# A two-layer encoder trunk: background work of the FFN's up stage queued behind each product's copy and addition, left operands stepped by a schedule, and right-operand sums formed between rows

## The chip, the cores and the metric

The kernel runs on one core of a Trainium2 chip. The metric is the device time of one execution in microseconds (us); the figure given for a kernel is the median of several runs.

The engines are named as in the profile. PE is TensorE: its matmuls write PSUM, and its weight loads are PEld. DVE is VectorE and ACT is ScalarE. POOL is GpSimd. SP issues the DMAs. Each engine takes its own instructions in a fixed order, and semaphores hold an instruction back until its inputs and its output buffer are free.

## What is computed

A tensor of 1024 tokens by 1024 features runs through two layers. Each layer adds a mixer (a state-space group and a differential attention group) and then a gated FFN with a causal convolution over three tokens. The part that matters here:

```python
def _conv_gated_ffn(h, w_up, w_conv, b_conv, w_down):
    up = h @ w_up
    padded = jnp.pad(up, ((0, 0), (CONV_WIDTH - 1, 0), (0, 0)))
    conv = b_conv + sum(w_conv[j] * padded[:, j:j + seqlen] for j in range(CONV_WIDTH))
    gate = conv[..., :FFN_DIM]
    val = conv[..., FFN_DIM:]
    return (jax.nn.silu(gate) * val) @ w_down

    # in the layer loop (DEPTH = 2, D_MODEL = SEQ = 1024, FFN_DIM = 2816)
    x = x + jnp.concatenate([y_ssm, y_att], axis=-1) @ w_out[i]
    h = _rmsnorm(x, norm_ffn[i])
    x = x + _conv_gated_ffn(h, w_up[i], w_conv[i], b_conv[i], w_down[i])
```

## The kernel before, in words

**Arithmetic.** A float32 matmul is made of three fp32r matmuls. `mm3` (lines 449 to 451) multiplies the rounded part ("hi") and the remainder ("lo") of both operands: hi by hi, hi by lo, lo by hi. A hi part is an ACT copy with rounding (`act`, line 97). A lo part is a subtraction: on POOL for weights (`split`, line 240), on DVE for most right operands (`Pieces.put`, line 472).

**The up stage.** `h @ w_up` is done with seven products in place of eight (the Strassen-Winograd form of a 2 by 2 block product). For each of the 22 tiles `f` of 128 FFN columns, the left blocks are gate and value columns by two halves of the features, and the right blocks are two halves of the features by two halves of the tokens. The right operands are seven sets of 512 features by 512 tokens, held as hi and lo: blocks 11, 21 and 22, and the sums t1 = 12 - 11, t2 = 22 - t1, t3 = 22 - 12, t4 = t2 - 21. One product is 4 feature tiles times three matmuls, so 12 matmuls of 128 by 512. `up(f)` runs the products 11, 12, s2, s1, s3, 22, s4 in this order into four PSUM tiles: `upa` takes 11, s2 and s3, each added to what stands there; `upb` takes 12; `upc` takes s1 and then s4 on top; `upd` takes 22. In between, ACT copies `upa` out into `u0` or `u1` after each of its three products, and DVE adds `upb`, `upc`, `upd` and `upc` again (line 100). The second product into `upa` or `upc` must not begin before the copy or addition that reads the first.

**Background work.** `bg` is a list of generators. `bg.tick()` lets each do one step, and `up` ticks after each product, seven times for one `f`. A step's instructions are written at the point of the tick, and the framework's scheduler then merges them, engine by engine, with the products' own copies and additions. Two kinds run here:

- `gate(f)` starts when `up(f)` ends. It makes the convolution of the value half (`c1`: one ACT operation, two DVE operations of line 106), of the gate half (`c0`), the silu on ACT and the multiplication into `g` on DVE.
- After every odd `f` up to 17, `spill` makes the seven left operands of the down stage out of two `g` tiles: sums on DVE (lines 317, 318, 328, 334), hi on ACT and lo on DVE (line 346) into tiles `ao`, which SP then stores to DRAM. It is a pipeline of three: at each tick one operand is summed, the previous one is rounded, the one before that gets its lo part. So it lies over the second half of an even `f` and all of the next odd `f`, together with the next gate.

POOL meanwhile makes the weights' sums and lo parts, seven products ahead of their use (`W.depth = 7`).

**The way into the up stage.** The output projection (`wo`) finishes token tiles `X[t]` of 128 rows, t = 0 to 7. After each odd t, `norm_ffn(tp)` norms two of them (tp = 0 to 3): squares on ACT, a Newton iteration on small DVE operations (`nw`, `rstd`), a scaling into `hn` (line 106). PE transposes `hn` (line 504) into PSUM tiles `nt`, and `put` writes hi and lo parts. For tp = 0 and 1 (tokens 0 to 511) these are the blocks 11 and 21. For tp = 2 and 3, `three(k)` takes the transposed blocks 12 and 22 out of PSUM and forms t1, t2 and t3 in tiles `ta` and `tb`, subtracting the hi and lo parts of 11 one after the other; t4 follows likewise (line 1320), on POOL for tp = 2. The products 11 and 12 of f = 0 and f = 1 need only tokens 0 to 511 and are run first, in front of

```python
        ups = [up(0), up(1)]
        for e in ups:
            next(e)
        bg.finish()
        W.fences.pop(0)
```

so all four norms are finished before `up(0)` goes on with its product s2.

Of the kernel before, what the change touches and what calls it, by code (L numbers as in the profile page):

```python
# [46 lines left out]
DN_ORDER = ["11", "12", "s2", "s3", "s1", "22", "s4"]  # L47
PARTNER = {"11": "11", "12": "21", "s4": "22", "22": "t4", "s1": "t1", "s2": "t2", "s3": "t3"}
# [3 lines left out]
def trunk_kernel(ctx: ExitStack, tc: tile.TileContext, A: dict, out: bass.AP, dbg: dict):  # L52
# [46 lines left out]
    def tt(o, a, b, op):  # L99
        V.tensor_tensor(o, a, b, op=op)  # L100
# [189 lines left out]
    class Seven:  # L290
# [49 lines left out]
        def spill(self, dst):  # L340

            todo, summed, rounded = list(DN_ORDER), None, None
            while todo or summed or rounded:
                if rounded:
                    (n, v, d), rounded = rounded, None
                    self.eng(n).tensor_tensor(d[:, 512:1024].bitcast(F32R), v, d[:, 0:512], op=SUB)  # L346
                    store(dst[n], d)
                if summed:
                    (n, v), summed = summed, None
                    d = s4("ao")  # L350
                    act(d[:, 0:512].bitcast(F32R), v, AF.Copy)
                    rounded = n, v, d
                if todo:
                    n = todo.pop(0)
                    summed = n, self.value(n)
                yield
# [131 lines left out]
    def norm_rows(xs, g, os, ps=None):  # L488

        n = len(xs)  # L490
        ss, y = few("ss", n), few("rstd", n)
        for i, (x, o) in enumerate(zip(xs, os)):
            squares.append(act(o, x, AF.Square, accum_out=ss[:, i:i + 1]))
# [4 lines left out]
    def turned(hs, k):  # L498

        n = 128 * len(hs)  # L500
        ps = bgt("nt")
# [685 lines left out]
    for l in range(DEPTH):  # L1187
# [86 lines left out]

        def norm_ffn(tp):

            rows_ = X[2 * tp:2 * tp + 2]
            hs = [s4("hn") for _ in rows_]
            norm_rows(rows_, gf, hs, mmt("nw") if tp == 3 else None)
            for s in range(2):  # L1280
                dma(xm[2 * tp + s], rows_[s])
            yield 1
            c, half = 256 * (tp % 2), tp // 2
            sums = G if tp == 2 else V

            def old(n, k, q):
                return B[n].tile(k, c)[q].rearrange("p (k n) -> p k n", k=2)[:, :, c:c + 256]

            def three(k):

                ta, tb = s4("ta"), s4("tb")
# [14 lines left out]
            if half == 0:  # L1306
# [256 lines left out]
```

## Time and profile before

| what | value |
|---|---|
| median of 3 runs | 2508.43 us (2503.97 to 2510.72) |
| the profiled execution | 2508.28 us, of which its span is 2506.5 us |
| PE busy | 2332.5 us (93% of the span) |
| PEld busy | 1931.1 us (77%) |
| DVE busy | 1758.8 us (70%) |
| ACT busy | 1111.8 us (44%) |
| POOL busy | 1163.4 us (46%) |
| mean granted TensorE clock | 0.979 of full speed |

The span is the time from the first to the last instruction. Busy time of PE counts overlapping matmuls once. A matmul's duration is longer than its share of the engine, since the next one starts before it ends; how fast PE goes is read from the distance between starts.

### The profile page before, as it was taken

The page shows a single profiled execution, that of the slowest core. Times are in us where ns is not written, and L with a number is a line of the kernel's source. Part 1 is how long each engine was busy: PE and PEld are TensorE (multiplying, and loading weights), DVE is VectorE, ACT ScalarE, POOL GpSimd, SP SyncE. Part 2 cuts the span into 40 slices and gives each one's busy share as a digit, 9 for nine tenths or more (in the row PEclk, how much of TensorE's full clock was granted, in tenths as well). Part 3 has the DMA queues.
Part 4 walks back from the last instruction along what each step waited for, and adds up shares of the span by engine and source line. Part 5 has one row for each costly group of instructions (what it writes and reads, how often), then busy time and mean ns, then how long its engine had stood idle before and what let it go on. Part 6 is the DMA issues. An engine that isn't in the chain of part 4 may idle for free. (4 is left out here: it accounts for less than half of the span.)

```text
span 2506.5 us, 34993 instructions
## 1 busy us (share of the span) xinstructions
PE 2332.5 (93%) x12180; PEld 1931.1 (77%) x12180; DVE 1758.8 (70%) x3273; ACT 1111.8 (44%) x2164; POOL 1163.4 (46%) x853
## 2 busy tenths in 40 slices
PE   5899999997999999999998999999979999999998
PEld 4777987785887777777787788877858777787776
DVE  7986567658777878456589775675677787864645
ACT  4455256434555555323135642754255555552221
POOL 3110011035777878778022101012277788878750
PEclk8999999999999999999999999999989999999999
DMA  6344741421344445786134447214114444549651
GB/s 179 119 115 116 196 120 47 149 82 51 109 148 130 161 134 176 296 305 236 53 101 153 116 135 216 70 51 156 68 42 143 135 155 139 167 161 367 225 180 68
DMA packets 295753, 361.42 MB, mean 144 GB/s; under 512 B 43160, under 2 KB 230136, under 8 KB 295576
## 3 DMA queue, kind: packets, MB, share of 16 engines
q1 hardware_dynamic: 295576, 359.18, 43.7%
q8 instruction: 97, 1.59, 0.3%
q14 instruction: 80, 0.66, 0.1%
HBM read 235.36 MB, written 123.73 MB: 143 GB/s over the span
## 5 line engine op out<-in xcount | busy, mean ns | idle before, releaser
L240 POOL TENSOR_TENSOR op<-st,op 128x512 fp32r<-128x512 f32 x112 | 169.5, 1541 | 886.5 <-ACT op L97 812.9
L240 POOL TENSOR_TENSOR op<-wu,op 128x512 fp32r<-128x512 f32 x220 | 325.1, 1499 | 160.9 <-ACT op L97 159.0
L106 DVE SCALAR_TENSOR_TENSOR c<-u,cv,c 128x1023 f32<-128x1023 f32 (+1 forms) x176 | 230.1, 1309 | 56.9 <-ACT c L97 52.8
L449 PE MATMUL rw<-op,hTh 128*128 128x256 f32 x768 | 228.8, 298 | 10.3 <-ACT hTh L97 3.5
L450 PE MATMUL rw<-op,hTh 128*128 128x256 f32 x768 | 225.8, 294 | 1.6 <-POOL op L240 1.6
L451 PE MATMUL rw<-op,hTl 128*128 128x256 f32 x768 | 224.1, 292 | 0.0
L100 DVE TENSOR_TENSOR xf<-xf,dnc 128x512 f32<-128x512 f32 (+1 forms) x160 | 124.7, 792 | 132.7 <-PE dnc L451 121.1
L240 POOL TENSOR_TENSOR op<-w,op 128x512 fp32r<-128x512 f32 x124 | 175.3, 1427 | 20.6 <-ACT op L97 20.5
L97 ACT ACTIVATE c<-u,cv 128x1024 f32<-128x1024 f32 x88 | 106.6, 1211 | 150.7 <-DVE u L100 144.0
L240 POOL TENSOR_TENSOR op<-wd,op 128x512 fp32r<-128x512 f32 x106 | 138.3, 1331 | 66.7 <-ACT op L97 66.7
L449 PEld LDWEIGHTS rw<-op,hTh 128*128 128x128 f32 x768 | 152.3, 198 | 12.9 <-ACT kr L97 4.6
L449 PE MATMUL dnc<-op,aop 128*128 128x512 f32 x360 | 146.0, 411 | 12.6 <-DVE xf L100 12.2
L450 PEld LDWEIGHTS rw<-op,hTh 128*128 128x128 f32 x768 | 152.2, 198 | 4.4 <-POOL op L240 2.3
L451 PEld LDWEIGHTS rw<-op,hTl 128*128 128x128 f32 x768 | 151.8, 198 | 0.7 <-issue 0.6
L450 PE MATMUL dnc<-op,aop 128*128 128x512 f32 x360 | 141.0, 392 | 0.0
L100 DVE TENSOR_TENSOR u<-u,upc 128x512 f32<-128x512 f32 x88 | 59.9, 681 | 115.3 <-ACT u L97 109.2
L97 ACT ACTIVATE u<-upa 128x512 f32<-128x512 f32 x132 | 78.0, 591 | 139.3 <-PE upa L451 137.2
L451 PE MATMUL dnc<-op,aop 128*128 128x512 f32 x360 | 139.1, 391 | 0.0
L97 ACT ACTIVATE op<-wu 128x512 fp32r<-128x512 f32 x220 | 128.9, 619 | 0.0
L346 DVE TENSOR_TENSOR ao<-g,ao 128x512 fp32r<-128x512 f32 x90 | 117.5, 1320 | 15.7 <-ACT ao L97 15.7
L97 ACT ACTIVATE op<-wd 128x512 fp32r<-128x512 f32 x106 | 62.2, 624 | 148.7 <-PE dnc L451 61.0
L97 ACT ACTIVATE e<-sc,anm 128x256 f32<-128x256 f32 (+7 forms) x128 | 94.1, 738 | 63.0 <-DVE anm L103 48.8
(346 smaller groups left out, 7124.0 us busy)
## 6 DMA issues: line engine op xcount, KB each, us to landing
wu<-in_w_up_dram SPq DMA_DIRECT2D x88, 512.0 KB
ad_s<-ao SPq DMA_DIRECT2D x72, 512.0 KB
aop<-ad_s SPq DMA_DIRECT2D x72, 512.0 KB
ad<-ao SPq DMA_DIRECT2D x54, 512.0 KB
aop<-ad SPq DMA_DIRECT2D x54, 512.0 KB
wd<-in_w_down_dram SPq DMA_DIRECT2D x44, 512.0 KB
st<-in_w_in_dram SPq DMA_DIRECT2D x32, 256.0 KB
st<-in_w_in_dram SPq DMA_DIRECT2D x16, 512.0 KB
```

Source lines behind the costliest of these rows:

```text
L97: return nc.scalar.activation(o, i, f, **kw)
L100: V.tensor_tensor(o, a, b, op=op)
L106: return V.scalar_tensor_tensor(o, a, s, b, op0, op1)
L240: eng.tensor_tensor(lo.bitcast(F32R), src, hi, op=SUB)
L346: self.eng(n).tensor_tensor(d[:, 512:1024].bitcast(F32R), v, d[:, 0:512], op=SUB)
L449: PE.matmul(o, l[0], r[0], start=first, stop=False, skip_group_check=go_on)
L450: PE.matmul(o, l[0], r[1], start=False, stop=False, skip_group_check=go_on)
L451: PE.matmul(o, l[1], r[0], start=False, stop=last, skip_group_check=go_on)
```

## The change

**Background.** A new function `behind()` ticks the background inside `tc.issue_after`: each instruction that the tick writes on ACT gets an order edge to the latest copy out of `upa`, each one on DVE an edge to the latest addition, so that the scheduler may not put it ahead of them. This holds once all norms are done. All ticks in `up` go through it.

**Left operands.** `spill` follows a table, `SPILL`: for each of nine ticks it lists which sums, hi and lo parts are made. The same 4 sums, 7 hi and 7 lo parts are made as before. The third and fourth ticks, which meet the convolutions of the next gate, are empty.

**Right operands.** The squares of a row tile are taken right after its last addition. For tp = 2 and 3 the sums t1, t2, t3 and t4 are formed between rows, before the transposition, in place in the `hn` tiles of tokens 0 to 511 (which are kept) and of tokens 512 to 1023, with t2 in the first of the two `X` tiles, whose store has been issued. Then all five blocks are transposed, so 10 groups of 8 transposes for these two tp where there were 4 of 8, through the wide PSUM tiles (`mmt`, two buffers). Every `put` now reads PSUM, all sums are on DVE.

**Order.** `up(0)` runs its products s2, s1, s3, 22 and s4 in two halves of 256 tokens, the first half as soon as tp = 2 is there, and the norms are finished after it.

```diff
+SPILL = [[("sum", "s1"), ("hi", "11")], [("sum", "s2"), ("lo", "11"), ("hi", "12")], [], [],
+         [("lo", "12"), ("sum", "s3"), ("hi", "s2")], [("lo", "s2"), ("sum", "s4"), ("hi", "s3")],
+         [("lo", "s3"), ("hi", "s1")], [("lo", "s1"), ("hi", "22"), ("hi", "s4")], [("lo", "22"), ("lo", "s4")]]
...
+            for step in SPILL:
+                for what, n in step:
+                    if what == "sum":
+                        o, p, q, op = sums[n]
+                        tt(o, p, q, op)
+                    elif what == "hi":
+                        d[n] = s4("ao")
+                        act(d[n][:, 0:512].bitcast(F32R), v[n], AF.Copy)
+                    else:
+                        tt(d[n][:, 512:1024].bitcast(F32R), v[n], d[n][:, 0:512], SUB)
+                        store(dst[n], d.pop(n))
                 yield
...
+            def put(n, src):
+                ps = mmt("nt") if tp > 1 else None
+                ps = [turned(src, k, ps and ps[:, 256 * k:256 * k + 512]) for k in (0, 2)]
                 for k in (0, 2):
-                    for n in ("11", "21"):
-                        B[n].put(k, 2, c, 256, turned(hs, k + 4 * (n == "21")))
+                    B[n].put(k, 2, c, 256, ps[k // 2])
...
+            for o, h, t2 in zip(ol, hs, e):
+                tt(o[:, lo], h[:, lo], o[:, lo], SUB)
+                tt(t2, h[:, hi], o[:, lo], SUB)
+            for o, h, t2 in zip(ol, hs, e):
+                tt(h[:, lo], h[:, hi], h[:, lo], SUB)
+            if tp == 2:
+                yield 1
+            for o, h, t2 in zip(ol, hs, e):
+                tt(o[:, hi], t2, o[:, hi], SUB)
+            yield 0 if tp == 2 else 2
...
+        def behind():
+
+            with ExitStack() as st:
+                for x in (emptied, added):
+                    if x and not any(e in bg.q for e in norms):
+                        st.enter_context(tc.issue_after(x[-1].ins))
+                bg.tick()
...
             product(a, "11", True)
-            act(u0[:, lo], a, AF.Copy)
-            bg.tick()
+            emptied.append(act(u0[:, lo], a, AF.Copy))
+            behind()
...
+            ws = W.take(5) if f == 0 else [None] * 5
+            for q, qn in ((0, 256), (256, 256)) if f == 0 else ((0, 512),):
+                v, x, y = slice(q, q + qn), slice(q, q + qn), slice(512 + q, 512 + q + qn)
+                product(a, "s2", False, ws[0], q, qn)
+                emptied.append(act(u0[:, y], a[:, v], AF.Copy))
+                behind()
...
+                product(a, "s3", False, ws[2], q, qn)
+                emptied.append(act(u1[:, x], a[:, v], AF.Copy))
+                added.append(tt(u1[:, y], u1[:, x], c[:, v], ADD))
+                behind()
...
         for e in ups:
             next(e)
-        bg.finish()
-        W.fences.pop(0)
-        for f in range(NF):
+        for e in ups[0]:
+            pass
+        bg.finish(*norms)
+        for f in range(1, NF):
```

Three places show what moves. The first is on DVE in f = 5 of the first layer, from the addition of `upb` to the addition of `upc` after which product s4 may begin. `w7` holds the sums s1 and s2, `g` the tiles of the gates (s3 and s4 are made in place in them), `ao` a left operand, `c0` and `c1` the convolutions. Before:

```order
L100 TENSOR_TENSOR u0_7479<-u0_7479,upb_7478 128x512
L328 TENSOR_TENSOR g_7271<-g_7271 128x512
L106 SCALAR_TENSOR_TENSOR c0_7533<-u0_7338,cv_4185,c0_7533 128x1022
L346 TENSOR_TENSOR ao_7530<-w7_7500,ao_7530 128x512
L346 TENSOR_TENSOR ao_7555<-g_7271,ao_7555 128x512
L346 TENSOR_TENSOR ao_7578<-w7_7500,ao_7578 128x512
L334 TENSOR_TENSOR g_7421<-g_7421,w7_7500 128x512
L100 TENSOR_TENSOR g_7580<-g_7580,c1_7503 128x1024
L100 TENSOR_TENSOR u1_7480<-u1_7480,upc_7557 128x512
```

Now (other line numbers, the same operations):

```order
L103 TENSOR_TENSOR u0_7580<-u0_7580,upb_7579 128x512
L109 SCALAR_TENSOR_TENSOR c1_7598<-u1_7480,cv_4185,c1_7598 128x1022
L109 SCALAR_TENSOR_TENSOR c0_7623<-u0_7432,cv_4185,c0_7623 128x1023
L103 TENSOR_TENSOR ao_7576<-g_7516,ao_7576 128x512
L109 SCALAR_TENSOR_TENSOR c0_7623<-u0_7432,cv_4185,c0_7623 128x1022
L103 TENSOR_TENSOR g_7363<-g_7363 128x512
L103 TENSOR_TENSOR ao_7646<-w7_7554,ao_7646 128x512
L103 TENSOR_TENSOR g_7516<-g_7516,w7_7554 128x512
L103 TENSOR_TENSOR u1_7627<-u1_7627,upc_7648 128x512
```

The gate's multiplication has moved behind the addition of `upc`; of the left operands five operations stood in front of it, now four stand there, with three convolution operations that ran earlier before.

The second place is on ACT at the start of f = 6. Before, the convolutions of f = 5 (`c1`, `c0`) stand ahead of the copy out of `upa` after product 11 (`op` are weights' hi parts):

```order
L97 ACTIVATE op104_7649<-wu_7367 128x512
L97 ACTIVATE c1_7666<-u1_7480,cv_4185 128x1024
L97 ACTIVATE c0_7691<-u0_7479,cv_4185 128x1024
L97 ACTIVATE u0_7647<-upa_7645 128x512
L97 ACTIVATE op105_7673<-wu_7513 128x512
```

Now:

```order
L100 ACTIVATE op104_7742<-wu_7461 128x512
L100 ACTIVATE u0_7741<-upa_7739 128x512
L100 ACTIVATE c1_7760<-u1_7627,cv_4185 128x1024
L100 ACTIVATE op105_7767<-wu_7608 128x512
L100 ACTIVATE c0_7785<-u0_7580,cv_4185 128x1024
```

The copy comes first, the convolutions behind it.

The third place is on DVE on the way into the up stage, at tp = 3. Before, for one of two pairs of feature tiles:

```order
L100 TENSOR_TENSOR ta_6763<-nt_6765,b11h_6370 128x512
L100 TENSOR_TENSOR ta_6763<-ta_6763,b11l_6371 128x512
L100 TENSOR_TENSOR ta_6763<-nt_6770,ta_6763 128x512
L100 TENSOR_TENSOR tb_6764<-nt_6770,tb_6764 128x512
L472 TENSOR_TENSOR bt1l_6605<-ta_6763,bt1h_6604 128x2x256
L472 TENSOR_TENSOR bt2l_6601<-ta_6763,bt2h_6600 128x2x256
L472 TENSOR_TENSOR bt3l_6609<-tb_6764,bt3h_6608 128x2x256
L472 TENSOR_TENSOR b22l_6613<-nt_6770,b22h_6612 128x2x256
```

Now, with sums for tp = 3 among the lo parts of tp = 2 (`xr` is the `X` tile that holds t2):

```order
L103 TENSOR_TENSOR hn_6353<-hn_6571,hn_6353 128x512
L103 TENSOR_TENSOR u0_6708<-u0_6708,upb_6707 128x512
L478 TENSOR_TENSOR bt3l_6735<-nt_6725,bt3h_6734 128x2x256
L103 TENSOR_TENSOR xr6_5865<-hn_6571,hn_6353 128x512
L103 TENSOR_TENSOR hn_6571<-hn_6571 128x512
L478 TENSOR_TENSOR bt3l_6739<-nt_6725,bt3h_6738 128x2x256
L478 TENSOR_TENSOR bt4l_6765<-nt_6755,bt4h_6764 128x2x256
L103 TENSOR_TENSOR hn_6352<-xr6_5865,hn_6352 128x512
```

The sums now read two tiles of rows, and each lo part reads a PSUM tile.

## Rows read from the trace of the kernel before

**Rows 1.** Windows, first layer: length; PE, PEld, DVE, ACT, POOL busy; clock; DMA share.

```profile
575.80:637.80 62.00, 46.48 (x194) 35.11 (x193) 51.29 (x67) 31.59 (x54) 42.23 (x29) 0.92 0.14 43
637.80:1031.00 393.20, 383.21 (x1668) 311.49 (x1667) 294.65 (x277) 207.48 (x321) 313.74 (x221) 1.00 0.44 147
```

**Rows 2.** Tile u of the whole span: who waited for it (us, times).

```profile
  PE upc L449: 18.9, 20
  PEld upa L449: 10.8, 18
```

**Rows 3.** Timeline of PE, f = 5 into f = 6: start, us, what, [idle before].

```profile
712.74 0.39 PE L451 MATMUL upd<-bt4h,op 128*128 128x512 f32 x1
714.04 0.50 PE L449 MATMUL upc<-b22h,op 128*128 128x512 f32 x1 [0.92 <-DVE u L100]
...
716.89 0.39 PE L449 MATMUL upa<-b11h,op 128*128 128x512 f32 x1
...
719.62 0.39 PE L449 MATMUL upb<-b21h,op 128*128 128x512 f32 x1
...
722.11 0.39 PE L451 MATMUL upb<-b21h,op 128*128 128x512 f32 x1
722.68 0.50 PE L449 MATMUL upa<-bt2h,op 128*128 128x512 f32 x1 [0.18 <-ACT u L97]
```

**Rows 4.** Timeline of DVE over the first of these two stalls.

```profile
703.59 0.68 DVE L100 TENSOR_TENSOR u<-u,upb 128x512 f32<-128x512 f32 x1
704.18 1.19 DVE L328 TENSOR_TENSOR g<-g 128x512 f32<-128x512 f32 x1
705.29 1.28 DVE L106 SCALAR_TENSOR_TENSOR c<-u,cv,c 128x1022 f32<-128x1022 f32 x1
706.48 0.68 DVE L346 TENSOR_TENSOR ao<-w,ao 128x512 fp32r<-128x512 f32 x1
707.09 1.78 DVE L346 TENSOR_TENSOR ao<-g,ao 128x512 fp32r<-128x512 f32 x1
708.79 1.77 DVE L346 TENSOR_TENSOR ao<-w,ao 128x512 fp32r<-128x512 f32 x1
710.49 1.77 DVE L334 TENSOR_TENSOR g<-g,w 128x512 f32<-128x512 f32 x1
712.18 1.21 DVE L100 TENSOR_TENSOR g<-g,c 128x1024 f32<-128x1024 f32 x1
713.32 0.67 DVE L100 TENSOR_TENSOR u<-u,upc 128x512 f32<-128x512 f32 x1
```

**Rows 5.** Timeline of POOL in the same stretch.

```profile
706.61 1.71 POOL L334 TENSOR_TENSOR wu<-wu,w 128x512 f32<-128x512 f32 x1
```

**Rows 6.** Timeline of ACT before the two stalls.

```profile
710.44 0.60 ACT L97 ACTIVATE u<-upa 128x512 f32<-128x512 f32 x1 [1.38 <-PE upa L451]
...
720.90 1.21 ACT L97 ACTIVATE c<-u,cv 128x1024 f32<-128x1024 f32 x1 [1.95 <-DVE u L100]
722.05 0.58 ACT L97 ACTIVATE u<-upa 128x512 f32<-128x512 f32 x1
```

**Rows 7.** The page: group of line 346 on DVE, count, mean ns.

```profile
L346 DVE TENSOR_TENSOR ao<-g,ao 128x512 fp32r<-128x512 f32 x90 | 117.5, 1320 | 15.7 <-ACT ao L97 15.7
```

**Rows 8.** Timeline of PE: matmuls of 256 columns, transposes, the longest wait.

```profile
63.02 0.28 PE L450 MATMUL rw<-op,hTh 128*128 128x256 f32 x1
63.14 0.28 PE L451 MATMUL rw<-op,hTl 128*128 128x256 f32 x1
...
550.42 1.04 PE L504 MATMUL nt<-ident,hn 128*128 128x128 f32 x8
...
592.85 0.66 PE L504 MATMUL nt<-ident,hn 128*128 128x128 f32 x2 [6.58 <-DVE rstd L103]
```

**Rows 9.** Groups of DVE in the window 572.2 to 621.6: dearest and cheapest SBUF group.

```profile
L472 DVE TENSOR_TENSOR bt3l<-tb,bt3h 128x512 fp32r<-128x512 f32 x4 | 6.0, 1506 | 0.0
...
L100 DVE TENSOR_TENSOR ta<-ta,b11l 128x512 f32<-128x512 f32 x4 | 2.8, 688 | 0.1
```

More of the change, by code (lines that the diff above doesn't have):

```diff
@@ L496, in norm_rows, with turned @@
             scaled.append(stt(o, x, y[:, i:i + 1], g, MUL, MUL))
-    def turned(hs, k):
+    def norm_rows(xs, g, os, ps=None):
+        ss = few("ss", len(xs))
+        for i, (x, o) in enumerate(zip(xs, os)):
+            norm_square(x, o, ss, i)
+        norm_scale(xs, g, os, ss, ps)
+    def turned(hs, k, ps=None):
         n = 128 * len(hs)
-        ps = bgt("nt")
+        ps = ps or bgt("nt")
         for q in range(2):
@@ L1310, in norm_ffn @@
+            if tp < 2:
+                yield 2
+                for n, v in (("11", lo), ("21", hi)):
+                    put(n, [h[:, v] for h in hs])
                     yield
                 return
-            xs = []
-            for k in (0, 2, 4, 6):
-                if k < 4:
-                    xs.append(three(k))
-                if k > 2:
-                    B["t4"].put(k - 4, 2, c, 256, xs[(k - 4) // 2], eng=sums)
-                if 0 < k < 6:
-                    for q in range(2):
-                        sums.tensor_tensor(xs[k // 2 - 1], xs[k // 2 - 1], old("21", k - 2, q), op=SUB)
+            ol = held.pop(tp - 2)[0]
@@ L1321, in norm_ffn @@
+            yield 0 if tp == 2 else 2
+            src = {"t1": [o[:, lo] for o in ol], "t2": e, "t3": [h[:, lo] for h in hs],
+                   "t4": [o[:, hi] for o in ol], "22": [h[:, hi] for h in hs]}
+            for group in (("t2", "t1", "t3", "t4", "22") if tp == 2 else (("t2",), ("t1", "t3"), ("t4",), ("22",))):
+                for n in ((group,) if tp == 2 else group):
+                    put(n, src[n])
                 yield
@@ L1352, in trunk_kernel @@
             tt(X[t], X[t], ps, ADD)
+            if t % 2 == 0:
+                held[t // 2] = [s4("hn"), s4("hn")], few("ss", 2)
+            hs, ss = held[t // 2]
+            norm_square(X[t], hs[t % 2], ss, t % 2)
             bg.tick()
@@ L1355, in trunk_kernel, with product @@
                 e = norm_ffn(t // 2)
-                next(e)
-                bg.add(e)[1] = 2
-        def product(o, n, first):
-            w = W.take()[0]
+                norms.append(bg.add(e))
+                norms[-1][1] = next(e)
+        def product(o, n, first, w=None, c=0, cn=512):
+            w = w or W.take()[0]
             for k in range(4):
-                mm3(o, tuple(v[:, 128 * k:128 * k + 128] for v in w), B[PARTNER[n]].get(k, 0, 512),
+                mm3(o[:, c:c + cn], tuple(v[:, 128 * k:128 * k + 128] for v in w), B[PARTNER[n]].get(k, c, cn),
                     first and k == 0, k == 3, not first)
```

111 lines of the change are left out of this document (47 added, 64 removed).

## The prediction, made before the changed kernel was run

> **What bounds the kernel now.** I read the page first: PE is busy for 93% of the span, so time can only come out of the stretches in which PE waits. Then I put windows over the stage that the change touches. The up stage of a layer falls into two parts [rows 1]. From 575.8 to 637.8 us, f = 0 and f = 1 run while the last norms are still coming in. There DVE is busy for 51.3 of 62.0 us, and the granted clock of PE is 0.92 of full speed. From 637.8 to 1031.0 us the other twenty f run at clock 1.00, PE is busy for 383 of 393 us and DVE for 295. The second layer repeats both parts (61.9 and 393.2 us), so each gain counts twice.
>
> Next I asked who waits in the steady part. Product s4 (`upc`) was held 20 times, 10 in each layer, by an addition on DVE, and a product into `upa` 18 times by ACT's copy [rows 2]. The timeline of PE shows one pair of these stalls [rows 3]. The first matmul of s4 starts 1.30 us after the last of product 22, where starts otherwise lie 0.23 us apart (twelve in 719.62 - 716.89 = 2.73 us): 1.07 us lost. The product then takes 2.85 us, 0.12 more. At 722.11 the step is 0.57 us, 0.34 too long; with the same 0.12 for the restart a pair of stalls costs 1.65 us. There are 9 pairs in a layer, one for each spill, and one further stall of about 1.2 us at f = 21. Both layers: 18 x 1.65 + 2 x 1.2 = 32 us. The window agrees: 139 products of 2.73 us are 379.5 us of its 393.2.
>
> Why is the addition late? On DVE it stands behind four lo parts and sums of the spill and the gate's multiplication, one after the other without a gap, and starts at 713.32 [rows 4]. ACT had the value ready at 710.44 + 0.60 = 711.04 [rows 6]. The second stall is ACT's: its copy at 722.05 stood behind a convolution that had itself waited 1.95 us for DVE [rows 6].
>
> **Part 1: the copy ahead of the convolutions.** The new order on ACT puts the copy first. That takes the 0.34 + 0.12 us out of each of 18 pairs: 8.3 us. What is late next is the convolution, by one copy of 0.6 us; behind it waits the gate, and nothing on PE.
>
> **Part 2: the spill by schedule.** It makes the same sums and parts, at other places, so the total work of DVE stays. What counts is what stands between the addition of `upb` and that of `upc`. Product s4's turn comes at 712.74 + 0.23 = 712.97, four products of 2.73 us after product 12 ends (702.05); product 11 ends at 699.3. The new order there is: first tap of c1, addition of `upb`, three more taps, four operations of the spill among them, addition of `upc`. ACT's copy (0.60) and c1 (1.21) come first, so the first tap runs from about 701.3 to 702.6 and the addition to 703.3. Three taps of 1.28 us [rows 4] lead to 707.1. To end by 712.97, the last addition (0.67) must start at 712.3. So the four spill operations have 5.2 us, 1.3 us each.
>
> Their price is the open question. These operations read two SBUF tiles. In [rows 4] five of them took 1.19, 0.68, 1.78, 1.77 and 1.77 us, 1.44 on average; the 90 lo parts averaged 1.32 [rows 7]. The dear ones meet POOL: the one that began at 707.09 ended at 708.87, 0.55 us after POOL's operation ended at 708.32 [rows 4, 5], as if it had waited for that end. I take 1.4 us, between the two averages. Then the stall is 4 x 1.4 - 5.2 = 0.4 us and 0.12 for the restart, where it was 1.19. The other path to the same addition (sum s3, its rounding, the silu, a weight's rounding, the copy, all in ACT's order) comes out at the same size. So a pair gains 1.65 - 0.5 = 1.15 us, 18 pairs 20.7, and with half of the two single stalls 22 us. The ends: at 0.68 us apiece no stall is left, 32 us; at 1.78 the stall is 1.92 + 0.12 us, and the 18 pairs lose 7 us against now.
>
> **Part 3: the sums between rows.** In one layer's first part, DVE now has 22 operations on two SBUF tiles, from 0.69 to 1.51 us a group [rows 9] seven groups, and 25.1 us together, 1.14 on average, and 16 that read PSUM at 0.68, as the addition at 703.59 does [rows 4]: 36 us. Afterwards there are 16 sums on two SBUF tiles, 20 lo parts that read PSUM (13.6 us) and three more, shorter, additions for the halves of f = 0 (1.6 us). I price the sums at 0.9 us, between the cheapest group and the present average, because six POOL operations for t4 leave this stretch: 14.4 us. That is 29.6 in place of 36 us, and DVE, which PE waits for here (6.58 us at once for the Newton iteration [rows 8]), ends 6 us earlier.  Both layers: 12 us. The ends: all sums at 0.68 give 10 us a layer; all at 1.78 lose 8 us a layer.
>
> On PE the part adds 48 transposes a layer at 1.04 / 8 = 0.13 us at most [rows 8], 6.2 us, and cuts 60 matmuls of 512 columns into 120 of 256 at 0.12 us [rows 8] in place of 0.23: 0.8 us. Both lie in PE's waits: fourteen products are 38.2 us, 80 transposes 10.4, so 49.4 of the 62 us are filled and the gain can't pass 12.6 us a layer. Without that cover they would cost 14 us over both layers.
>
> **What costs nothing.** The squares are the same ACT operations, earlier, on an engine that is busy for half of this window (31.6 of 62 us [rows 1]). On SP, loads of weights queue behind the spill's last store, which comes a few us later in the new order; the ring runs seven products ahead, 19 us. Holding four more `hn` tiles could delay a load for want of a buffer; the same 19 us cover that. t2's place in an `X` tile waits for that tile's store, issued two tiles earlier.
>
> **The sum.** The profiled execution took 2508.28 us (span 2506.5), the median of the runs is 2508.43, so nothing has to be shifted. 2508.3 - 22 - 12 = 2474 us.
>
> **Rivals.** A difference under 0.3% (7.5 us) can't be told from no change.
>
> - *All stalls go.* If the four operations mostly miss POOL (0.68 us), both terms reach their upper ends: 32 + 20 = 52, 2456 us. For it: [rows 4] holds such a one at 0.68. Against: POOL is busy for 314 of 393 us [rows 1].
> - *DVE's stall stays in the steady part.* With 1.65 us apiece the pair's stall is 1.5 us; with ACT's part and f = 0 and 1 won, about 14 us remain: 2494 us. For it: three of five operations in [rows 4] cost 1.77 or more.
> - *The transposes wait for PSUM.* Ten groups pass through two wide tiles, one of which the Newton iteration of tp = 3 holds at first. A group needs about 1.0 (transposes), 0.6 (hi) and twice 0.7 us (lo). If PE, which takes its instructions in order, stands at each group, the 12 us go, and with half of part 2 the time is 2500 us or a little more: no change.
> - *Slower, by POOL.* If each DVE operation on two SBUF tiles waits for a POOL operation in both places, 1.78 us apiece, part 2 loses 7 us and part 3 16: 2530 us. Priced alike in both places at m, the gain is 164 - 104 m us: nothing at 1.58, slower beyond 0.3% from 1.65. Against it: the averages of 1.32 and 1.14, and fewer such operations in part 3 (16 for 22).
>
> The Trainium skill's page "SBUF — State Buffer", section "Who interferes with whom", has this rival as a rule: a DVE instruction with two SBUF inputs and a GpSimd instruction that reads SBUF exclude each other for a whole instruction, and one with at most one SBUF input does not contend. The trace agrees where it can be read: the operation of 1.78 us that ended 0.55 us behind POOL's. By that rule alone, with POOL never idle, the time would be the 2530 us of the last rival.
>
> That the order edges do nothing is ruled out by the new order itself: the copies and additions did move.
>
> **How the numbers follow.** Forecast (2462 to 2488): 0.57. All stalls gone: 0.17. DVE's stall stays: 0.15. No change: 0.06. Slower: 0.05. The first three are faster by over 0.3%, 0.89; within 0.3% 0.06; slower 0.05. The range that leaves out no more than 2 in 10 reaches from most of the first rival to most of the second: 2449 to 2498.
>
> **What would show it.** Right: the step from product 22 to s4 in odd f falls from 1.30 to 0.3 to 0.7 us, the 0.57 us step goes to 0.23, and two f take 38.3 to 38.8 us in place of 39.8; PE's wait of 6.58 us is broken up, and f = 1 ends some 6 us earlier against the last `wo` matmul. Wrong in part 2: an operation of the spill that begins within a POOL operation directly ahead of the addition of `upc`, or ACT's copy late behind a silu. Wrong in part 3: PE waiting for `nt` tiles at every group of transposes, or the granted clock of this part below 0.92. It would also be wrong if the ring of weights ran dry, seen as PE waiting for POOL's lo parts.

## The result, and the profile after

The changed kernel takes 2464.2 us (median of 4 runs, 2463.1 to 2465.1) against 2506.2 us (4 runs, 2503.7 to 2510.7) of the kernel before: a ratio of 0.9829, 95% interval 0.9814 to 0.9843, or 42 us less. The forecast was 2474 us with a range of 2449 to 2498. The profiled execution took 2464.45 us (span 2462.7); its span is 43.8 us shorter.

The windows of the changed kernel over the same two parts of the up stage as in [rows 1], from the last `wo` matmul to the first of f = 2, and on to product s4 of f = 21:

```profile
575.90:629.01 53.11, 48.86 (x310) 43.38 (x309) 38.74 (x66) 28.34 (x50) 30.83 (x23) 1.00 0.17 50
629.01:1009.47 380.46, 378.25 (x1670) 312.98 (x1668) 272.69 (x279) 208.50 (x323) 302.31 (x222) 1.00 0.45 151
```

Between the same marks the kernel before took 62.2 and 394.7 us:

```profile
575.59:637.80 62.21, 46.69 (x195) 35.25 (x194) 51.50 (x68) 31.67 (x54) 42.23 (x29) 0.92 0.14 43
637.80:1032.52 394.72, 383.63 (x1669) 311.49 (x1668) 295.34 (x278) 208.75 (x323) 315.26 (x222) 1.00 0.45 148
```

So a layer gains 9.1 us on the way into up and 14.3 us in the steady part, and the second layer repeats it (9.0 and 14.2). These are 46.6 us. The span fell by 2.8 us less, since waits came back behind them (below) and stretches that no edit touches differ from run to run.

The waits for tile `u` (us, times), which answer to [rows 2]:

```profile
  PE upc L455: 5.5, 4
```

Of 20 waits at `upc` 4 are left, one in f = 0 and one at f = 21 of each layer, and `upa` is not in the list any more. The timelines of f = 5 show why, for DVE (answers to [rows 4]):

```profile
694.96 1.28 DVE L103 TENSOR_TENSOR ao<-g,ao 128x512 fp32r<-128x512 f32 x1
...
697.36 0.70 DVE L103 TENSOR_TENSOR g<-g 128x512 f32<-128x512 f32 x1
697.98 0.68 DVE L103 TENSOR_TENSOR ao<-w,ao 128x512 fp32r<-128x512 f32 x1
698.58 0.68 DVE L103 TENSOR_TENSOR g<-g,w 128x512 f32<-128x512 f32 x1
700.79 0.69 DVE L103 TENSOR_TENSOR u<-u,upc 128x512 f32<-128x512 f32 x1 [1.53 <-issue]
```

for POOL:

```profile
696.21 1.29 POOL L243 TENSOR_TENSOR op<-w,op 128x512 fp32r<-128x512 f32 x1 [0.51 <-ACT op L100]
700.29 1.29 POOL L243 TENSOR_TENSOR op<-w,op 128x512 fp32r<-128x512 f32 x1 [2.79 <-ACT op L100]
```

for ACT:

```profile
700.11 0.59 ACT L100 ACTIVATE u<-upa 128x512 f32<-128x512 f32 x1
```

and for PE:

```profile
702.45 0.39 PE L455 MATMUL upc<-b22h,op 128*128 128x512 f32 x1
```

The four spill operations took 1.28, 0.70, 0.68 and 0.68 us, 0.83 on average over this f and over all 18 pairs: POOL was idle from 697.50 to 700.29. DVE then stood idle for 1.53 us. The row names nobody who ended this wait; ACT's copy, which the addition reads, was ready at 700.70, 0.09 us before the addition began. The addition ended at 701.48, 0.97 us before product s4's turn at 702.45.

**What came back.** At s4 of f = 21 the step on PE grew from 1.49 to 2.60 us, and PE waits at the entry of the down stage, where it did not wait before:

```profile
1009.47 0.50 PE L455 MATMUL upc<-b22h,op 128*128 128x512 f32 x1 [2.21 <-DVE u L103]
...
1016.70 0.50 PE L455 MATMUL dn<-op,aop 128*128 128x512 f32 x1 [0.81 <-DMA aop<-ad]
...
1023.74 0.50 PE L455 MATMUL dnc<-op,aop 128*128 128x512 f32 x1 [1.98 <-DVE xf L103]
```

Their cause is read from ACT before, and then from ACT, DVE and SP of the changed kernel:

```profile
1030.63 0.63 ACT L97 ACTIVATE op<-w 128x512 fp32r<-128x512 f32 x1 [4.78 <-POOL w L321]
```

```profile
1007.58 0.63 ACT L100 ACTIVATE op<-w 128x512 fp32r<-128x512 f32 x1 [5.44 <-POOL w L324]
1008.11 0.58 ACT L100 ACTIVATE u<-upa 128x512 f32<-128x512 f32 x1
```

```profile
1008.73 0.69 DVE L103 TENSOR_TENSOR u<-u,upc 128x512 f32<-128x512 f32 x1 [7.71 <-ACT u L100]
1009.33 1.22 DVE L103 TENSOR_TENSOR g<-g,c 128x1024 f32<-128x1024 f32 x1
...
1023.00 0.69 DVE L103 TENSOR_TENSOR xf<-xf,dnc 128x512 f32<-128x512 f32 x1 [9.78 <-DMA xf<-xm]
```

```profile
1010.57 0.32 SPq L130 DMA_DIRECT2D gd<-g  x1
...
1011.48 3.26 SPq L1477 DMA_DIRECT2D aop<-ad_s  x4
1014.83 2.21 SPq L1511 DMA_DIRECT2D xf<-xm  x4
```

Both kernels raise the number of weights that are held ahead (the ring, `W.depth`) from 7 to 9 within f = 21. In both, ACT's copy stands behind a weight's rounding that waits for POOL, 4.78 us before and 5.44 us now. The gate's multiplication of f = 20, whose silu ended at 1002.14, is held by the edge behind the addition of `upc` until 1009.33. Its store `gd` goes out at 1010.57, and the loads of the down stage (`aop`, `xf`) stand behind it in SP's order. Before, this store went out at 1027.20, 5.3 us ahead of product s4 of f = 21; now it is 1.1 us behind it.

### The profile page after: what moved, and what is told of

It is laid out like the page before. It is cut to its first block, busy times and chain, and to the rows that moved or that the text cites. A ratio compares the mean times of both kernels' runs of the same rounds, so it can differ in the third digit from the quotient of the medians.

```text
span 2462.7 us, 35332 instructions
## 1 busy us (share of the span) xinstructions
PE 2322.6 (94%) x12396; PEld 1946.8 (79%) x12396; DVE 1690.5 (69%) x3275; ACT 1106.1 (45%) x2160; POOL 1114.6 (45%) x841
## 3 DMA queue, kind: packets, MB, share of 16 engines
q8 instruction: 98, 1.61, 0.3%
## 5 line engine op out<-in xcount | busy, mean ns | idle before, releaser
L243 POOL TENSOR_TENSOR op<-wu,op 128x512 fp32r<-128x512 f32 x220 | 298.9, 1375 | 94.2 <-ACT op L100 94.2
L109 DVE SCALAR_TENSOR_TENSOR c<-u,cv,c 128x1022 f32<-128x1022 f32 (+1 forms) x176 | 226.0, 1308 | 52.5 <-ACT c L100 51.6
L243 POOL TENSOR_TENSOR op<-w,op 128x512 fp32r<-128x512 f32 x124 | 159.8, 1296 | 179.5 <-DVE rstd L106 92.2
L100 ACT ACTIVATE u<-upa 128x512 f32<-128x512 f32 (+1 forms) x136 | 79.5, 585 | 269.9 <-PE upa L457 269.9
L103 DVE TENSOR_TENSOR u<-u,upc 128x512 f32<-128x512 f32 (+1 forms) x92 | 61.1, 664 | 176.4 <-ACT u L100 101.3
L100 ACT ACTIVATE op<-wu 128x512 fp32r<-128x512 f32 x220 | 133.9, 622 | 11.4 <-POOL op L243 11.4
L103 DVE TENSOR_TENSOR ao<-g,ao 128x512 fp32r<-128x512 f32 x90 | 124.6, 1400 | 0.0
L979 DVE TENSOR_REDUCE am<-sc 128x1 f32<-128x256 f32 (+7 forms) x128 | 93.9, 751 | 31.0 <-PE sc L977 30.8
```

Source lines behind the costliest of these rows:

```text
L100: return nc.scalar.activation(o, i, f, **kw)
L103: return V.tensor_tensor(o, a, b, op=op)
L109: return V.scalar_tensor_tensor(o, a, s, b, op0, op1)
L243: eng.tensor_tensor(lo.bitcast(F32R), src, hi, op=SUB)
L979: V.tensor_reduce(out=m[:, c:c + 1], in_=sv, axis=AX.XY, op=ALU.max)
```

## The experiments

All times are compared with the kernel before on the same chip. "Way" is the time from the last `wo` matmul to f = 2, "steady" that from f = 2 to product s4 of f = 21, both per layer (first, second), "step" the distance of starts at that s4, and "entry" the waits at the entry of the down stage that the kernel before does not have, as the excess of the steps over 0.23 us.

| kernel | way | steady | step | entry | median | ratio (95% interval) |
|---|---|---|---|---|---|---|
| before | 62.2, 62.2 | 394.7, 394.7 | 1.49 | 0 | | |
| changed | 53.1, 53.1 | 380.5, 380.5 | 2.60 | 3.1, 2.1 | 2464.2 | 0.9829 (0.9814 to 0.9843) |
| edges alone | 62.2, 62.4 | 391.3, 391.6 | 2.61 | 2.4, 0.5 | 2511.3 | 1.0002 (0.9992 to 1.0012) |
| table alone | 62.2, 62.2 | 405.4, 405.3 | 1.48 | 0, 0 | 2533.6 | 1.0092 (1.0075 to 1.0109) |
| edges and table | 62.2, 62.2 | 380.5, 380.5 | 2.60 | 2.3, 2.4 | 2488.7 | 0.9910 (0.9896 to 0.9925) |
| way alone | 54.6, 53.1 | 394.7, 394.7 | 1.48 | 0, 0 | 2485.8 | 0.9906 (0.9891 to 0.9920) |
| no edges on DVE | 54.7, 53.1 | 380.5, 380.5 | 2.62 | 0, 0 | 2461.7 | 0.9811 (0.9788 to 0.9833) |
| no edges on ACT | 53.1, 53.1 | 379.3, 379.3 | 1.49 | 3.3, 2.2 | 2464.0 | 0.9819 (0.9793 to 0.9846) |
| f = 0 whole | 58.2, 58.1 | 380.4, 380.5 | 2.60 | 0.8, 0.6 | 2477.0 | 0.9870 (0.9843 to 0.9897) |
| last f mended | 54.6, 53.1 | 378.1, 378.1 | 0.23 | 0, 0 | 2455.9 | 0.9789 (0.9766 to 0.9811) |
| POOL reads | 53.1, 53.1 | 381.0, 380.7 | 2.60 | 2.3, 2.2 | 2468.2 | 0.9832 (0.9815 to 0.9849) |
| POOL fills | 54.7, 53.1 | 381.0, 380.7 | 2.62 | 3.3, 1.6 | 2473.0 | 0.9839 (0.9812 to 0.9866) |
| halves alone | 63.6, 63.6 | 380.5, 380.5 | 2.61 | 1.1, 2.2 | 2492.1 | 0.9928 (0.9911 to 0.9945) |
| edges, pause | 62.2, 62.2 | 384.0, 383.7 | 2.61 | 0.4, 0.7 | 2494.2 | 0.9927 (0.9908 to 0.9946) |

The windows tell more than the medians: stretches that no edit touches differ by some us from run to run (last section).

**1. Edges alone.** The kernel before with `behind()`, the old spill and the old norms:

```diff
+            emptied.append(act(u0[:, lo], a, AF.Copy))
+            behind()
...
+            added.append(tt(u0[:, lo], u0[:, lo], b, ADD))
+            behind()
```

> The kernel before, with the order edges alone (old spill, old norms). Theory: the change is two parts that add, and in the steady part the edges do the work, since with them alone the stretch on DVE between the additions of upb and upc already holds three taps and four spill operations as in the changed kernel. Then the window from the start of f = 2 to product s4 of f = 21 falls from 394.7 to 380.5 to 383 us a layer, DVE's stalls at upc go, and, because the gate's multiplication of f = 20 now stands behind the addition of upc, about 3 us come back at the entry of the down stage: 2480 to 2485 us. Rival: the table is needed. On ACT two roundings of the spill still stand among the convolutions, so the taps come 0.6 us later and a stall of 0.5 to 1 us stays at each upc: 390 us a layer, 2495 us.

There is no change in the time, and the steady part gains only 3.1 to 3.4 us a layer. The theory missed; the rival's stall is there, but by another path. DVE, ACT and PE of f = 5 in this kernel:

```profile
701.17 1.63 DVE L346 TENSOR_TENSOR ao<-g,ao 128x512 fp32r<-128x512 f32 x1
702.73 1.77 DVE L328 TENSOR_TENSOR g<-g 128x512 f32<-128x512 f32 x1
...
706.22 1.27 DVE L106 SCALAR_TENSOR_TENSOR c<-u,cv,c 128x1022 f32<-128x1022 f32 x1
...
709.66 0.69 DVE L100 TENSOR_TENSOR u<-u,upc 128x512 f32<-128x512 f32 x1 [1.58 <-ACT u L97]
```

```profile
707.60 1.03 ACT L97 ACTIVATE g<-c 128x1024 f32<-128x1024 f32 x1 [1.35 <-DVE c L106]
...
709.04 0.59 ACT L97 ACTIVATE u<-upa 128x512 f32<-128x512 f32 x1
```

```profile
710.41 0.50 PE L449 MATMUL upc<-b22h,op 128*128 128x512 f32 x1 [0.90 <-DVE u L100]
```

The addition is late because it waits 1.58 us for ACT's copy. The copy stands behind the silu (`g<-c`), the silu waits for the last tap on DVE, and the taps stand behind two spill operations of 1.63 and 1.77 us. The stall at s4 is as long as in [rows 3]; only ACT's short stall at `upa` is gone.

**2. Table alone.** The kernel before with `SPILL` and the new `spill` in place of the old one, plain ticks:

```diff
-            todo, summed, rounded = list(DN_ORDER), None, None
...
+            for step in SPILL:
+                for what, n in step:
```

> The kernel before, with the table for the left operands alone (no order edges). Theory: three operations in place of nine stand between the additions of upb and upc, so DVE's stalls go, but ACT's copy out of upa still stands behind the two convolutions, and its 9 stalls of about 0.5 us a layer stay: the window from f = 2 to s4 of f = 21 is about 385 us a layer in place of 394.7, nothing is given back at the down stage (the multiplication of f = 20 is not held), 2487 us. Rival, if the edges are what counts: the additions of upb are now late behind four taps, the stall only moves, and the window stays above 390 us, 2497 us or more.

The theory fails: it is 0.9% slower (23 us), 10.7 us a layer in the steady part. That lies within the rival's bounds (above 390 us a layer, 2497 us or more), but the path is another than the rival's. ACT, DVE and PE at the start of the next f:

```profile
704.23 1.21 ACT L100 ACTIVATE c<-u,cv 128x1024 f32<-128x1024 f32 x1 [5.08 <-DVE u L103]
705.38 0.58 ACT L100 ACTIVATE u<-upa 128x512 f32<-128x512 f32 x1
```

```profile
697.83 1.18 DVE L103 TENSOR_TENSOR ao<-g,ao 128x512 fp32r<-128x512 f32 x1
698.93 1.77 DVE L103 TENSOR_TENSOR g<-g 128x512 f32<-128x512 f32 x1
700.63 1.77 DVE L103 TENSOR_TENSOR g<-g,w 128x512 f32<-128x512 f32 x1
...
703.52 0.67 DVE L103 TENSOR_TENSOR u<-u,upc 128x512 f32<-128x512 f32 x1
```

```profile
706.01 0.50 PE L455 MATMUL upa<-bt2h,op 128*128 128x512 f32 x1 [2.60 <-ACT u L100]
```

The bunched spill operations now run ahead of the last addition into `u0`, the convolution of `u0` waits 5.08 us for it, and ACT's copy stands behind the convolution. The stall at s4 is gone, but the one at `upa`, 0.34 us too long before, has become a step of 2.98 us, in 9 pairs a layer.

**3. Edges and table, and 4. the way alone.** Experiment 3 has the edits of 1 and 2 together. Experiment 4 is the changed kernel with the old spill and without the edges:

```diff
-            with ExitStack() as st:
-                for x in (emptied, added):
...
+            bg.tick()
```

> Edges and table, without the part on the way into up (old norms, f = 0 not in halves). Theory of two parts that add: the window falls by 14.2 us a layer as in the changed kernel, about 3 us come back behind it: 2506 - 28.5 + 3 = 2481 us. By the forecast's own price (1.4 us for each spill operation, half of the stall at f = 21 gone) it is 2506 - 22 = 2484 us. Rival: part of the gain of the steady part comes from the new way in (a free DVE and full clock at f = 2): the window stays above 384 us a layer and the time above 2488 us.

> The way into up alone: sums between rows, f = 0 in halves, norms finished behind it; the old spill and no order edges. Theory of two parts that add: 9 us a layer from the last wo matmul to f = 2 (62.2 to 53.1 us), and nothing given back at the down stage, since the multiplication of f = 20 is not held: 2506 - 18 = 2488 us. By the forecast's price 12 us: 2494 us. Rival: the gain is only moved, because f = 2 starts with the background of f = 0 and 1 still to be done: the window from f = 2 on grows beyond 396 us and the time stays above 2496 us.

The two parts do add: 14.2 us a layer here, 9.1 us there in the second layer (7.6 in the first, where the granted clock was 0.97), and by the ratios 22.6 and 23.6 us in all. What comes back at the down stage comes with the edges (experiments 1 and 3) and not with the way alone. The theory had 25 and 18 us. The windows fit it; in experiment 4 they hold 16.7 of the 23.6 us, and the rest lies outside of them, where kernels differ by some us without an edit (last section).

**5. No edges on DVE, and 6. none on ACT.** The changed kernel, with one list taken out of the loop (`added` in 5, `emptied` in 6); that of 5:

```diff
-                for x in (emptied, added):
+                for x in (emptied,):
```

> The changed kernel without the order edges on DVE (those on ACT stay). New theory: each part by itself only moves the wait on, since ACT and DVE take their instructions in order; with the table, one of the two edges is enough to break the chain convolution - copy. ACT's copy stands ahead of the convolutions, so a late addition of upc on DVE delays only the gate: the window from f = 2 to s4 of f = 21 stays at 380.5 to 382 us a layer, and because the multiplication of f = 20 is no longer held behind the addition of upc, the step at s4 of f = 21 falls from 2.60 to 1.5 us and the step of 2.3 us in the down stage goes: 2458 to 2462 us. Rival (the forecast's split): the ACT edges are worth the 0.46 us of their own stall, 4 us a layer, and DVE's the other 10: the window goes back to about 390 us, 2483 us.

> The changed kernel without the order edges on ACT (those on DVE stay). New theory: with the addition of upc ahead of the spill on DVE, the convolution of c0 no longer waits for it, so ACT's copy behind both convolutions is there in time (product 12 gives it 2.73 us): window 380.5 to 382 us a layer, the stalls at f = 21 and in the down stage stay, 2463 to 2467 us. Rival (the forecast's part 1): the 0.46 us of ACT's stall come back 9 times a layer: window 384.6 us, 2472 us.

The new theory holds: with the table, the edges of one engine do all of it. With DVE's alone not even the 0.46 us of ACT's stall come back, since the addition that its convolution waits for is in time. One point missed in both expectations: the longer step at s4 of f = 21 stays without DVE's edges and goes without ACT's (1.49), so it is ACT's edges that make it. The waits at the entry go without DVE's edges and stay without ACT's, as expected.

**7. f = 0 in whole products, and 11. the halves without the sums between rows.**

```diff
-            for q, qn in ((0, 256), (256, 256)) if f == 0 else ((0, 512),):
+            for q, qn in ((0, 512),):
...
-        for e in ups[0]:
-            pass
         bg.finish(*norms)
```

Experiment 11 keeps the halves and takes the norms from the kernel before, with their transposes in wide tiles:

```diff
-                tt(o[:, lo], h[:, lo], o[:, lo], SUB)
...
+                nt = mmt("nt")
+                p12, p22 = turned(hs, k, nt[:, 0:512]), turned(hs, k + 4, nt[:, 512:1024])
...
+                tt(x1, p12, old("11", k, 0), SUB)
```

> The changed kernel with f = 0 in whole products, so all norms are finished before its product s2, and the sums between rows kept. Theory: the forecast priced only the sums (6 us a layer of DVE); the other 3 of the 9 us are the halves, which give PE 5 half products (6.8 us) to do while the last two rows are summed and turned. Then the way from the last wo matmul to f = 2 is 56 to 60 us in place of 53.1, 2470 to 2478 us. Rival a: the halves are worth nothing, DVE's sums alone set the end: 53 to 54 us, 2464 to 2466 us. Rival b: the halves are the whole gain: 62 us or more, 2482 us.

> The changed kernel with the norms of the kernel before (squares, sums and lo parts as there, t4 of tp = 2 on POOL; only the transposes go through the wide PSUM tiles), so f = 0 in halves without the sums between rows. With f = 0 whole and the new sums the way from the last wo matmul to f = 2 was 58.2 us (62.2 before, 53.1 with both). Theory that the two add: the halves take 5 us from 62.2: 57 us, 2471 to 2474 us. Rival a, as in the steady part each needs the other: DVE's old sums (51 us of work) end so late that the halves only move the wait: 60 us or more, 2478 us or more. Rival b, the halves are enough: 53 to 55 us, 2464 to 2467 us.

The windows of the way of 7 and then of 11:

```profile
577.76:635.96 58.20, 51.56 (x251) 42.90 (x249) 38.76 (x63) 28.66 (x48) 30.98 (x23) 0.91 0.15 46
```

```profile
576.71:640.33 63.62, 48.15 (x254) 40.77 (x253) 54.53 (x70) 31.84 (x55) 45.21 (x29) 0.87 0.14 42
```

The sums alone give 4.0 us of the 62.2, with DVE at 38.8 us of work; the halves alone lose 1.4, with DVE at 54.5; both together give 9.1. So the halves pay only when DVE is free to feed them, which was rival a of the last expectation. In the changed kernel the granted clock is 1.00 over this stretch; with either part alone it stays at 0.91 and 0.87, as it was 0.92 before. This is a second way in which the two parts together can pay. In experiment 7 PE waits 3.96 us at one place; from 596.7 to 607.0 us the granted clock is 0.50, the lower level, and a group of eight transposes takes 1.94 us there. In the changed kernel the longest wait is 1.88 us and such a group takes 1.06:

```profile
597.19 1.94 PE L517 MATMUL nt<-ident,hn 128*128 128x128 f32 x8 [3.96 <-DVE bt3l L478]
```

```profile
610.53 1.06 PE L517 MATMUL nt<-ident,hn 128*128 128x128 f32 x8 [1.88 <-DVE bt3l L478]
```

How much of the difference is waiting and how much the clock, no run separates.

**8. The last f mended.** No DVE edges while f = 21 runs; the ring of weights goes from 7 to 9 entries after up instead of within f = 21:

```diff
-                for x in (emptied, added):
+                for x in (emptied, added) if f < NF - 1 else (emptied,):
...
-                W.depth = NW
-                W.pump(W.pos + NW)
...
+        W.depth = NW
         last = l == DEPTH - 1
```

> The changed kernel, with two edits for the last f: no DVE edges while f = 21 runs, and the ring of weights raised from 7 to 9 entries after up has ended, not in the middle of f = 21. Theory: the edges gave back 1.1 us at s4 of f = 21 and 2 to 3 us at the entry of the down stage in each layer (the store of f = 20's gate is late, and SP's loads stand behind it), and the jump of the ring makes ACT's copy wait for POOL. Both go: the step at s4 of f = 21 falls from 2.60 to about 0.3 us, the step of 2.3 us is gone, 4.5 to 5 us a layer, 2454 to 2457 us. Rival: the weights of the down stage are late in turn (POOL has to make the same sums and lo parts a little later), and PE waits for them in the first two groups: no gain, 2462 to 2468 us.

The theory holds. The step is 0.23 us, there is no wait at the entry, and 378.1 us are 139 products of 2.72 us, so nothing is left to win there. The ratio is 0.9789 against 0.9829 of the changed kernel, 8 us by the medians and 10 by the ratios (their intervals just do not overlap): the fastest version here. The two edits were not run apart; that the step needs the second one follows from experiment 5, where it stayed at 2.62 us without any DVE edges.

**9. POOL reads, and 10. POOL fills.** Added work of no use on POOL, put where it had been idle beside the last three of the four spill operations; that of 9 is shown, and 10 has six `G.memset(z, 0.0)` in place of the four operations of the last line:

```diff
+                        if n == "12":
+                            z = wk("zz", 256)
+                            G.tensor_tensor(z, d[n][:, 512:768], d[n][:, 0:256], op=SUB)
+                            for _ in range(4):
+                                G.tensor_tensor(z, z, z, op=SUB)
```

> The changed kernel with added work on POOL that computes nothing of use: per spill, one operation of 128 x 256 that reads the lo and hi part of left operand 12 as soon as it is made, and four that read SBUF (128 x 256, a scratch tile with itself), so that POOL is busy in the 2.8 us in which it was idle before (697.5 to 700.3 us, f = 5) while DVE makes sum s3, the lo part of s2 and sum s4 at 0.68 to 0.70 us. Theory: these operations were cheap (0.83 us on average, forecast 1.4) because POOL was idle. Now each waits for an operation of POOL: 1.2 us or more on average, 1.5 us of idle time in front of the addition of upc are used up, and a stall of 0.5 to 1.5 us comes back at s4 in each of 18 pairs: 2475 to 2490 us. Rival: POOL has no part in it, the cheap ones are cheap by their tiles: 0.68 us as now, window 380.5 us a layer, 2462 to 2466 us.

> The control: the same first operation on POOL, and behind it six fills of 128 x 256 that read nothing from SBUF, in place of the four operations that read it. Theory (a POOL operation that reads SBUF excludes a DVE operation on two SBUF tiles): sum s3, lo of s2 and sum s4 stay at 0.68 to 0.75 us apart from one that can meet the first operation, no stall comes back, window 380.5 to 381.5 us a layer, 2463 to 2467 us. Rival (any busy POOL slows DVE, or the added POOL work makes the weights late): the same loss as with the operations that read, 2475 us or more.

With reads, DVE's four operations of f = 5, and POOL:

```profile
691.27 1.28 DVE L103 TENSOR_TENSOR ao<-g,ao 128x512 fp32r<-128x512 f32 x1
...
693.66 1.50 DVE L103 TENSOR_TENSOR g<-g 128x512 f32<-128x512 f32 x1
695.08 1.10 DVE L103 TENSOR_TENSOR ao<-w,ao 128x512 fp32r<-128x512 f32 x1
696.10 1.10 DVE L103 TENSOR_TENSOR g<-g,w 128x512 f32<-128x512 f32 x1
697.89 0.69 DVE L103 TENSOR_TENSOR u<-u,upc 128x512 f32<-128x512 f32 x1 [0.69 <-POOL zz L365]
```

```profile
693.32 1.29 POOL L243 TENSOR_TENSOR op<-w,op 128x512 fp32r<-128x512 f32 x1
694.58 3.79 POOL L365 TENSOR_TENSOR zz<-zz 128x256 f32<-128x256 f32 x4
```

With fills:

```profile
701.71 1.50 DVE L103 TENSOR_TENSOR g<-g 128x512 f32<-128x512 f32 x1
703.13 0.68 DVE L103 TENSOR_TENSOR ao<-w,ao 128x512 fp32r<-128x512 f32 x1
```

```profile
701.37 1.29 POOL L243 TENSOR_TENSOR op<-w,op 128x512 fp32r<-128x512 f32 x1
702.60 2.16 POOL L365 MEMSET zz<- 128x256 f32 x6
```

The price of the operations is as the theory has it: 1.24 us on average beside POOL operations that read, and 0.68 for each of the two beside fills. Its time is not: apart from 0.2 us at f = 9 of the first layer, in both kernels, no stall came back. 4 x 1.24 = 4.98 us is still within the 5.2 us that the forecast had found free, and DVE's idle time in front of the addition only shrank from 1.53 to 0.69 us.

The addition ended 0.18 us before s4's turn in both kernels, where it had 0.97 us, although the four operations averaged 1.24 us in one and 1.04 in the other. What they share is sum s3 (`g<-g`), at 1.50 us in place of 0.70: the added first operation moved one of POOL's own lo parts onto it, so for this sum the fills are no control. Its rounding stands ahead of the silu and the copy on ACT, so its 0.8 us reach the addition in full; the 0.42 us each of the two operations behind it only fill idle time. The medians of both kernels spread over 9 and 15 us and say nothing beyond the windows.

**12. Edges and a pause.** The kernel of experiment 1 and two empty ticks after the second step of the old pipeline:

```diff
                 yield
+                if n == "12":
+                    yield
+                    yield
```

> Order edges, the old pipeline of sum, rounding and lo part, and two empty ticks after its second step: of the table only the pause at the convolutions of the next gate. Theory: with the edges alone ACT's copy of s3 was late because it stands behind the silu, which waited for taps that stood behind the spill's operations on DVE. The pause takes these operations out of the taps' way, so the silu and the copy are in time; five spill operations in place of four then stand ahead of the addition of upc, 3.5 to 6.0 us where 5.2 are free: the window from f = 2 to s4 of f = 21 is 381 to 388 us a layer, 2483 to 2498 us. Rival: the pause is not what the table does, its order of sums is: 390 us or more, as with the edges alone, 2503 us or more.

The steady part takes 384 us, within the theory's range: of the 11 us a layer that separate the edges alone from edges and table, the pause gives 7.3 and 7.9. A step of 0.45 us stays at s4.

## Why the forecast held, and where it was off

The changed kernel came out 10 us below the forecast. Both terms were too small by some 6 us (28.5 measured for 22, 18 for 12), and 5.2 us that came back at the entry of the down stage had no term at all. That these errors offset each other in part is luck.

**The copy ahead of the convolutions (part 1, 8.3 us).** The size was right: with the old spill the edges won 3.4 + 1.1 = 4.5 us a layer, once the longer step at f = 21 is set aside, 0.5 us for each of 9 pairs. That it is a part of its own was wrong: with the table, DVE's edges give the same (experiment 6).

**The spill by schedule (part 2, 22 us).** It measured 28.5. The mis-sized term is the price of the four operations, "I take 1.4 us": it was 0.83, since POOL was idle beside three of them. The bound that the forecast drew, 1.3 us each before a stall returns, is not contradicted by the run that forced them to 1.24, but a price for each of the four alike is the wrong measure: experiments 9 and 10 show that sum s3 decides, through ACT. So the steady part went as in the rival "all stalls go": the nine pairs of a layer lost all 1.65 us each (14.2 + 1.1 of f = 21 = 15.3 us, with 9 x 1.65 = 14.9). The forecast ascribed this to the table. The table alone costs 10.7 us a layer, the edges alone win 3.3, both win 14.2: it is their joint effect, since each alone moves the wait on to the other engine's queue. The forecast's "other path", in ACT's order through the silu, was the one that decided this, in experiment 1 and in the changed kernel, where DVE waits for the copy. The forecast put it at a stall of the same 0.4 us; it ended 0.97 us early.

**f = 21.** "Half of the two single stalls" was the wrong sign: the step grew by 1.1 us. The copy stood behind a rounding that waits for POOL before, too, and without ACT's edges (experiment 6) the step is as long as it was. With them, a convolution that ran before ACT's copy after product 11 stands behind this copy, ahead of the first rounding of these weights, and POOL stands idle for that rounding 1.13 us longer (4.36 us before):

```profile
996.02 1.30 POOL L243 TENSOR_TENSOR op<-wd,op 128x512 fp32r<-128x512 f32 x1 [5.49 <-ACT op L100]
```

The chain behind it is later by some 1.1 us. Experiment 8 removed it by taking the jump of the ring out of f = 21.

**The sums between rows (part 3, 12 us).** It measured 18. The prices were right: the 12 sums in the window took 10.7 us, 0.89 on average (0.9 taken), the lo parts 0.68. The step that failed is the one from DVE's work to PE's time: 6 us a layer of DVE were equated with 6 us of PE, and the halves entered only as three more additions. DVE's work between the marks in fact fell by 12.8 us (51.5 to 38.7), partly because four of the sixteen sums run ahead of the last `wo` matmul; with f = 0 whole and the same work (38.8) PE gained only 4.0 us. The halves gave another 5.1 on top. The forecast took the clock of 0.92 as given; its rise to 1.00 had no term.

**What costs nothing.** Squares, the ring and the held tiles: no sign of them. The forecast looked at SP's queue for the weights only. It left out that an edge on DVE also holds what the tick issues as a DMA: the store of f = 20's gate, and behind it the loads of the down stage, 3.1 and 2.1 us.

**The rivals.** "DVE's stall stays" and "slower, by POOL" need the four operations at 1.65 us or more; they were at 0.83. "The transposes wait for PSUM" showed in part. PE has four waits on the way, of 0.44, 1.38, 0.55 and 1.88 us in the first layer. The third is s4's for DVE's addition; the other three, 3.7 us, are groups of transposes that begin as DVE ends a lo part out of an earlier `nt` tile. Seven of the ten groups did not wait, so the gain was cut and not lost.

## What to carry to other kernels

When two engines that work in order feed each other, price an order edge and a schedule together: one of them alone can move the same wait to the other engine's queue, and in the steady part of both layers the schedule alone lost 21 us and the edges alone won 6, where both together won 28. Before the end of a stage, release what an order edge holds back: its DMAs stand ahead of the next stage's loads in SP's order. Give an early piece of a product to PE only after its producer has been relieved.

## What the hardware showed that was not expected

**DVE and POOL.** A DVE operation on two SBUF tiles that begins within a POOL operation ended 0.55 us after it: 704.50 after 703.95 (experiment 1; POOL's row is below), 695.16 after 694.61 (experiment 9), 703.21 after 702.66 (experiment 10). In the changed kernel 108 of the 162 sums and lo parts of the left operands began so, and all ended 0.54 to 0.56 us after POOL's; the other 54 took 0.68 us. In the kernel before, 31 that began together with POOL's operation or 0.05 us before its end took 0.68 us as well. A blocked operation loses what is left of POOL's operation, not a fixed price, so its cost is set by when it starts.

```profile
702.34 1.61 POOL L334 TENSOR_TENSOR wu<-wu,w 128x512 f32<-128x512 f32 x1
```

The Trainium skill's page "SBUF — State Buffer", section "Who interferes with whom", says that such an operation contends with a GpSimd instruction that reads SBUF and not with one that only writes it; the fills of experiment 10 (0.68 us beside them) agree.

**The clock after one and the same wait.** In the down stage of the first layer PE waits 1.9 us for `xf` at one place in every kernel here. Windows of 7 us from that matmul on, in the kernel before and in that of experiment 8:

```profile
1193.90:1200.90 7.00, 6.99 (x31) 5.65 (x32) 3.60 (x4) 2.20 (x4) 3.61 (x3) 1.00 0.41 120
```

```profile
1166.40:1173.40 7.00, 6.96 (x24) 5.51 (x24) 3.63 (x4) 2.19 (x4) 2.26 (x2) 0.76 0.21 58
```

The wait was 1.92 us in the one and 1.91 in the other; behind it the granted clock was 1.00 and 0.76, part of the time at the lower of its two levels, and 24 matmuls were started in place of 31, 1.6 us of PE's work. Of the 14 profiles, 8 show 0.76 behind this wait and 6 show 1.00, whatever the edit; at the same place in the second layer, where PE waits 1.56 to 1.61 us, all 14 show 1.00. From the first matmul of the down stage to the next layer's first `wo`, which no edit touches but for the entry waits and, in experiment 8, the ring, the profiles took from 670.5 to 680.8 us. That is the noise in which differences of a few us between medians stand.
